# Attention on one core: other first loads, one last store, blank matmuls over a longer stretch, and a replanned order of work

## The chip, the cores and the metric

The kernel runs on one core of one Trainium2 chip. The metric is the device time of one execution in microseconds (us), as the median of several runs. A profile of one execution stands beside it; its times are counted from the start of its span, which is a little shorter than the device time. The engines are named as the profile names them: PE is TensorE's matmul, PEld its weight load, ACT is ScalarE, DVE is VectorE, POOL is GpSimd and SP is SyncE, which here only issues transfers (DMAs).

## The reference

Grouped-query attention over 8 batches, 8 query heads, 2 key/value heads, 1024 positions and a head dimension of 64, in float32:

```python
scores = scale * np.matmul(q_group, k_group.transpose(0, 1, 3, 2))
scores_max = np.max(scores, axis=-1, keepdims=True)
attn = np.exp(scores - scores_max)
attn = attn / (np.sum(attn, axis=-1, keepdims=True) + 1e-08)
output[:, q_start:q_end, :, :] = np.matmul(attn, v_group)
```

There are 64 (batch, query head) jobs. Each has a 1024 x 1024 score matrix, its exponential, a sum over each row, and a product with v. The inputs are small (0.1 times a normal draw), so the kernel leaves out the maximum.

## The kernel before, in words

A job's scores are made transposed, keys on the partitions. One score pair is two matmuls (line 754) of 128 keys against 512 queries each, for the two halves of the queries, and fills one of three slots in PSUM (the tiles sp0 to sp2, 128 x 1024 float32). A job has 8 such pairs, so there are 512 in all. Each pair's exponential is made by one of two engines:

- ScalarE makes it with one ACTIVATE of 128 x 1024 (line 767), which writes the bfloat16 tile pt.
- VectorE makes it in integer steps: a scale and offset to a 16-bit pattern (line 778, "yt"), and then for two pairs together a mask for the mantissa (line 785, "zt"), a mask for the exponent (line 792, "et") and a product (line 801). GpSimd makes the last 256 columns of some of the products (line 728). For all but the last two jobs, et and zt both go into the product with v, so a pair made this way costs TensorE two value matmuls where ScalarE's costs one.

The value product (line 819) has the exponential as weights and v, with a column of ones that gives the row sums, as the moving side (65 columns). Eight pieces of 128 queries make a job. Seven pieces at a time collect in one of two PSUM banks (ops0, ops1), and VectorE divides them by the sums (lines 875 and 884) into the ring tile ost, from which SP stores whole jobs (line 888). The last job collects in a score slot (line 840), and its store is cut in two halves, on SP's and on ScalarE's queue (line 852).

Queries and keys reach their transposed layout by DMA: GpSimd's queue casts them to bfloat16 in DRAM (lines 529 and 537), and SP's queue issues transposing loads (lines 562 and 572). The first job takes a faster path. Its q and k are loaded directly by four DMAs (line 594: k block 0 and then the upper half of q on ScalarE's queue, the lower half of q and then k blocks 1 to 3 on SP's), cast (line 615), transposed by matmuls against an identity (line 627) and copied out of PSUM (lines 636 to 638). After the first score pair, `rest_k0` transposes k blocks 1 to 3 and copies them with one VectorE instruction (line 643), and `swap_k0` makes the swapped-halves copy of k (line 653). Before the first real matmul, TensorE runs six blank matmuls of 512 columns and three of 128 on a zero tile (line 604).

The order of all of it is written out before the kernel is built, by a planner (the class Plan). It keeps a clock for each engine, made of constants for the durations (M_...), and at each step chooses for TensorE between a score for ScalarE ("A"), a score for VectorE ("D"), a piece of the value product ("V", up to GRAIN matmuls at once), a piece of the last job ("L"), a wait ("W") and a blank matmul of 128 columns ("F"). Where there is a choice it plays the alternatives forward over HORIZON and weighs ScalarE's and VectorE's idle time, TensorE's waste and its progress by W_A, W_D, W_P and W_LAG. MXD limits how many pairs of a job go to VectorE (two); every MORE-th job may have one more. M_START is the time at which the planner takes the first score to be possible. Blank matmuls within the plan are allowed until M_FILL and only before the first value matmul:

```python
elif t < M_FILL and s.pc == 0 and s.done == 0:
    kind = "F"
```

The planned events are then emitted in order of time, each engine having its own instruction stream and semaphores between them; transfers are emitted at set leads before the planned time of their use.

Of the kernel before, what the change touches and what calls it, by code (L numbers as in the profile page):

```python
# [8 lines left out]


M_START = 5400
M_SWAP = 1500
M_Q1 = 3400
M_QSTEP = 2700
M_WARM = 6400
M_FILL = 12000
M_DUMMY = 110
M_SEE = 51
M_PAIR = 226
# [15 lines left out]

M_GAP = 120
M_RUNWAY = 1800
M_BACK = 3000
M_WAIT = 150
M_TOL = 300  # L40

HORIZON = 9000
W_A = 1.0
W_D = .28
W_P = .3
W_LAG = 20
INF = float("inf")
PB = 7
NPIECE = 8
GRAIN = 3  # L50
MXD = 2
MORE = 12
TAIL = 2
# [59 lines left out]
class Plan:  # L113
# [5 lines left out]
    def __init__(self, nj, npt, nct, nyt):  # L119
        self.nj, self.npt, self.nct, self.nyt = nj, npt, nct, nyt  # L120

        self.last = (nj - 1) * NPIECE
        self.groups = [(i, min(i + PB, self.last)) for i in range(0, self.last, PB)]
        self.groups += [(self.last, self.last + NPIECE)]
        self.group_of = [g for g, (lo, hi) in enumerate(self.groups) for _ in range(lo, hi)]
        self.qready = [M_START] + [M_START + M_Q1 + M_QSTEP * j for j in range(nj - 1)]
        s = State()
        s.nxt = [0] * nj
        s.dcount = [0] * nj
        s.pcnt = [0] * nj  # L130
        s.pmax = [0] * nj
        s.a_of = [0] * nj
        s.mms = [8] * nj
        s.slot = [M_START, M_START, M_START + M_SWAP - 600]
        s.aq, s.dq = [], []
        s.out = [M_START, M_START]
        s.norms, s.gq = [], []
        s.tP = s.tA = M_START
        s.tD = M_START + M_SWAP
        s.tG = M_START + 9000  # L140
        s.endA, s.endD = s.tA, s.tD
        s.idleA = s.idleD = s.waste = 0
        s.mode = s.open = s.dlast = None
        s.dend = 0
        s.chains, s.heads, s.nch = [], {}, 0
        s.pc = s.done = s.a = s.used_p = s.used_c = 0
        s.lastp, s.left, s.spare = [INF] * 8, 8, None
        s.placed = 0
        s.end = False
        s.ev = []  # L150
        self.run(s)
# [118 lines left out]

    def pick_d(self, s):
        for j in range(s.a, min(self.nj, s.a + 3)):
            if s.nxt[j] < 8 and s.dcount[j] < MXD + (j % MORE == 1) and self.qready[j] <= s.tP:
                return j
        return None

    def choices(self, s):

        t, nj = s.tP, self.nj
        while s.a < nj and s.nxt[s.a] == 8:
            s.a += 1
        a = s.a
        cold = 2 if t < M_WARM else 1
        free = [x for x in (0, 1, 2) if s.slot[x] <= t]
        runway = s.tA - t + M_ACT * len(s.aq)
        slack = runway - cold * M_PAIR - M_PTAIL - (M_SWITCH if s.mode != "s" else 0)
        can_a = a < nj and len(s.aq) < 2 and self.qready[a] <= t and s.used_p < self.npt  # L290
        dj = None
        held = len({ch.id for ch in s.chains} | {x[1].id for x in s.gq})
        if not s.dq and held < self.nyt and (s.open or s.used_c < self.nct):
            if max(s.tD - t, 0) + sum(ch.left() for ch in s.chains) < M_BACK:
                dj = self.pick_d(s)
        s.free, s.dj = free, dj
        can = []
        kind = None
        if free:
            can += ["A"] * can_a + ["D"] * (dj is not None)  # L300
            if dj is not None:
                if not can_a:
                    kind = "D"
                elif len(free) > 1 or slack <= M_GAP or s.mode == "s":
                    other = min(s.slot[x] for x in (0, 1, 2) if x != free[0])
                    late = not s.aq and other > s.tA - M_PAIR - M_PTAIL + M_TOL
                    kind = "A" if late or slack <= M_PAIR else "D"
            elif can_a:
                full = len(free) > 1 or s.mode == "s"
                if slack <= M_GAP or (full and runway < M_RUNWAY):  # L310
                    kind = "A"
        pv = s.pc < self.last and (
            s.done > 0
            or (
                s.pcnt[s.pc // NPIECE] == 8
                and s.pmax[s.pc // NPIECE] <= t
                and s.out[self.group_of[s.pc] % 2] <= t
            )
        )
        wait = s.mode == "s" and any(t < x <= t + M_WAIT for x in s.slot)  # L320
        can += ["V"] * pv + ["W"] * (wait and (can_a or dj is not None))
        if kind is None:
            if wait and (dj is not None or (can_a and runway < M_RUNWAY + M_WAIT)):
                kind = "W"
            elif pv:
                kind = "V"
            elif s.left and a == nj and (free or s.spare is not None) and min(s.lastp) <= t:
                kind = "L"
            elif t < M_FILL and s.pc == 0 and s.done == 0:
                kind = "F"  # L330
            else:
                kind = "W"
        return kind, [x for x in can if x != kind]

    def turn(self, s, mode):
        if s.mode != mode:
# [4 lines left out]
    def pe(self, s, kind):  # L341
        t, nj = s.tP, self.nj
        if kind in "AD":
            self.turn(s, "s")
            sl = s.free[0]
            j = s.a if kind == "A" else s.dj
# [38 lines left out]
        elif kind == "L":  # L385

            if s.spare is None:
                s.spare = s.free[0]
                s.slot[s.spare] = INF
            self.turn(s, "v")  # L390
            c = min(range(8), key=lambda c: s.lastp[c])
            s.lastp[c] = INF
            s.left -= 1
            s.note(s.tP, "pvl", c, s.left, None)
            s.tP += NPIECE * M_MM
            if not s.left:
                s.norms.append((s.tP + M_PVTAIL, "rec", self.last, self.last + NPIECE))
        elif kind == "F":
            s.note(s.tP, "dummy", None, None, None)
            s.tP += M_DUMMY  # L400
            s.mode = "v"
        else:
            x = min([x for x in s.slot if x > t] + [max(s.tA, t) + 1, max(s.tD, t) + 1, t + 60])
            s.tP = max(x, t + 5)
            s.waste += s.tP - t
# [44 lines left out]
def kernel(  # L450
# [64 lines left out]
    warm = kvp.tile([128, HS], BF16, name="warm")  # L515
    ident = kvp.tile([128, 128], BF16, name="ident")
    nc.vector.memset(warm, 0.0)  # L517
    nc.vector.memset(va[:, :, :, :, D : D + 1], 1.0)
    kt, qt, qd, kd, vs = {}, {}, {}, {}, {}

    def cast_q(j):
# [65 lines left out]
    kt[(0, 0)] = ktp.tile([128, 2, HS], BF16, name="kt")  # L587
    qt[0] = qp.tile([128, 1, HS], BF16, name="qt")
    k0, q0 = kt[(0, 0)], qt[0]
    for e, x, lo, hi in (  # L590
        (nc.scalar, "k", 0, 1), (nc.sync, "q", 0, 2), (nc.scalar, "q", 2, NH), (nc.sync, "k", 1, NH)
    ):
        src = {"q": q, "k": k}[x][0, 0]
        e.dma_start(out=f32[x][:, lo:hi], in_=rows(src, True)[:, lo:hi])  # L594
    cast_q(1)
    make_identity(nc, ident)
    cast_q(2)
# [1 line left out]
    new_bank(0)  # L599
    new_bank(1)  # L600

    def dummy(n, cols):
        for _ in range(n):
            nc.tensor.matmul(  # L604
                ops[1][:, 0:cols], lhsT=warm[:, 0:128], rhs=warm[:, 0:cols], start=True, stop=True
            )

    dummy(6, HS)
    dummy(3, 128)

    def place(e, x, lo, hi):
        to, src = b16[x][:, lo:hi], f32[x][:, lo:hi]
# [27 lines left out]

    def rest_k0():
        turn("k", 1, NH, s2[:, 0])
        nc.vector.tensor_copy(out=k0[:, 0, 128:HS], in_=s2[:, 0, 128:HS])  # L643

    def swap_k0():
        for c in range(NH):
# [26 lines left out]
    for x in [e for e in plan.ev if e[1] == "norm"]:  # L673
        lo, hi = x[2]
        for j in range(NJ - 1):
            if lo < (j + 1) * NPIECE <= hi:
                ev.append((x[0] + 700, "store", None, j, None))
        if lo >= plan.last:
            ev.append((x[0] + 1, "half", 0, None, None))
            ev.append((x[0] + 2, "half", 1, None, None))  # L680
    order = {id(e): i for i, e in enumerate(ev)}
    ev.sort(key=lambda e: (e[0], order[id(e)]))

# [29 lines left out]
    for when, kind, x, j, c, *cols in ev:  # L713
# [110 lines left out]
                    stop=(i == len(every) - 1),  # L824
                )
        elif kind == "dummy":
            dummy(1, 128)
        elif kind == "pvl":
            b, h = divmod(NJ - 1, H)
            first = j == NC - 1  # L830
# [2 lines left out]
            for i in range(NPIECE):  # L833
# [5 lines left out]
                for n, (ci, p) in enumerate(every):  # L839
# [5 lines left out]
                        stop=(j == 0 and n == len(every) - 1),  # L845
                        skip_group_check=True,
                    )
        elif kind == "half":
            b, h = divmod(NJ - 1, H)
            r = plan.last % RING  # L850
            lo = x * 64
            (nc.scalar if x else nc.sync).dma_start(
                out=rows(out[b, h], True)[lo : lo + 64],
                in_=ost[lo : lo + 64, r : r + NPIECE, :].rearrange(
                    "p (s two) d -> p s (two d)", two=2
                ),
            )
        elif kind in ("rec", "norm"):
            lo, hi = x
            n = hi - lo  # L860
# [24 lines left out]
        elif kind == "store":  # L885
            b, h = divmod(j, H)
            r = j * NPIECE % RING
            ins = nc.sync.dma_start(
                out=rows(out[b, h], j == 0),
                in_=ost[:, r : r + NPIECE, :].rearrange("p (s two) d -> p s (two d)", two=2),  # L890
            )
            stores.append((when, ins))
# [30 lines left out]
```

The softmax here doesn't subtract the row's maximum and nothing guards it: scores larger than these inputs give would overflow.

## Time and profile before

| What | Value |
|---|---|
| Median of three runs | 365.02 us |
| Runs | 363.99, 365.12, 365.02 us |
| Profiled execution, device time | 363.19 us |
| Its span | 361.4 us |
| Its mean granted TensorE clock | 0.992 |
| PE, DVE, ACT busy | 97% each |
| POOL busy | 33% |
| ACTIVATE for the exponential | 378, mean 1057 ns each |
| VectorE's first step (yt) | 134, mean 1212 ns each |
| Value matmuls | 2976 from pt, 1056 from zt, 1040 from et |
| Score matmuls | 1024 |

Consecutive ACTIVATEs overlap in the record, so the mean duration of one is more than its share of the engine's busy time (348.6 us for 378). In a row of groups, the numbers after the bar are the busy time and the mean duration, and after the second bar the idle time just before these instructions with what ended it. In the chain of work that ended last and in the timeline, a row has its start, its length and what it is. In a table of stages, each row has the stretch and its length, then for PE, PEld, DVE, ACT and POOL the busy time and the number of instructions, then the granted TensorE clock as a share of full speed, the share of DMA time and the GB/s moved.

### The profile page before, as it was taken

Reading aid. Unit: us, or ns where it says so; the run is one execution under the profiler, and the core shown is the slowest. Engines: PE = TensorE matmul, PEld = TensorE weight load, DVE = VectorE, ACT = ScalarE, POOL = GpSimd, SP = SyncE. Lnnn points to the kernel's source line nnn. Section 1 sums busy time; section 2 is a strip of 40 time slices with the busy share of each in tenths; the row PEclk is TensorE's granted clock in tenths of the full one; section 3 lists DMA queues with packets and bytes.
Section 4 is the critical chain, followed back from the end, with each engine's and each line's share of the span. In section 5 each row is a group of like instructions: output and inputs, shape, how many; then the busy total and the mean of one; then the engine's idle time right before and its main releaser. Section 6 shows DMA issues by size and latency. Waiting matters only on the chain.

```text
span 361.4 us, 14113 instructions
## 1 busy us (share of the span) xinstructions
PE 349.0 (97%) x6213; PEld 222.2 (61%) x6213; DVE 349.4 (97%) x491; ACT 351.1 (97%) x382; POOL 120.8 (33%) x202
## 2 busy tenths in 40 slices
PE   7799999999999999999999999999999999999994
PEld 3256666566666666666665666666666666666664
DVE  4999999999999999999999999999999999999993
ACT  5999999999999999999999999999999999999994
POOL 4224443333334233343422333343324424432000
PEclk9989999999999999999999999999999999999998
DMA  6724767376696857469565676969468555853323
GB/s 160 134 41 77 188 108 147 84 139 143 110 161 115 166 103 162 99 123 172 125 143 108 124 137 111 171 119 150 107 129 149 122 118 122 175 132 48 88 61 89
DMA packets 89565, 44.82 MB, mean 124 GB/s; under 512 B 46032, under 2 KB 87888, under 8 KB 88272
## 3 DMA queue, kind: packets, MB, share of 16 engines
q1 hardware_dynamic: 86144, 33.37, 40.7%
q0 software_dynamic: 2992, 10.23, 21.1%
q8 instruction: 48, 0.79, 0.9%
q10 hardware_dynamic: 368, 0.33, 0.3%
q14 instruction: 13, 0.11, 0.1%
HBM read 25.17 MB, written 27.00 MB: 144 GB/s over the span
## 4 chain that ended last, share of the span: by engine, by line
PE 43%; DVE 35%; ACT 18%; issue 1%; DMA 1%; ACTq 0%; DVEq 0%
PE ops L819 24%; PE sp L754 18%; ACT pt L767 18%; DVE yt L778 16%; DVE zt L801 6%; DVE et L792 4%; DVE ost L884 4%; DVE zt L785 4%; DVE rec L875 1%; DMA q<-in_q_dram 1%; PE sp L840 1%; PE sp L627 0%; DVE kt L643 0%; DVE qt L637 0%; ACTq L594 0%
## 5 line engine op out<-in xcount | busy, mean ns | idle before, releaser
L767 ACT ACTIVATE pt<-sp 128x1024 bf16<-128x1024 f32 x378 | 348.6, 1057 | 2.2 <-PE sp L754 2.1
L819 PE MATMUL ops<-va,pt 128*128 128x65 bf16 x2976 | 186.2, 194 | 0.0
L754 PE MATMUL sp<-qt,kt 64*128 64x512 bf16 x1024 | 173.7, 384 | 6.3 <-ACT pt L767 3.4
L778 DVE TENSOR_SCALAR yt<-sp 128x1024 uint16<-128x1024 f32 x134 | 162.5, 1212 | 0.9 <-PE sp L754 0.9
L819 PEld LDWEIGHTS <-pt 128*128 128x128 bf16 x2976 | 136.3, 98 | 41.1 <-issue 41.1
L819 PE MATMUL ops<-va,zt 128*128 128x65 bf16 x1056 | 134.4, 195 | 0.0
L819 PE MATMUL ops<-va,et 128*128 128x65 bf16 x1040 | 128.5, 195 | 0.0
L728 POOL TENSOR_TENSOR zt<-yt,zt 128x256 bf16<-128x256 bf16 x102 | 68.2, 668 | 139.2 <-DVE zt L801 50.5
L819 PEld LDWEIGHTS <-et 128*128 128x128 bf16 x1040 | 84.8, 98 | 30.8 <-issue 30.8
L819 PEld LDWEIGHTS <-zt 128*128 128x128 bf16 x1056 | 88.2, 98 | 12.1 <-issue 12.1
L754 PEld LDWEIGHTS <-kt 64*128 64x128 bf16 x1024 | 45.5, 93 | 44.7 <-issue 22.1
L801 DVE TENSOR_TENSOR zt<-yt,zt 128x1536 bf16<-128x1536 bf16 (+1 forms) x67 | 67.8, 1012 | 0.0
L529 POOL DMA_DIRECT2D qd<-in_q_dram x62 | 35.5, 573 | 40.4 <-PE sp L754 38.0
L785 DVE TENSOR_SCALAR zt<-yt 128x2048 uint16<-128x2048 uint16 x67 | 45.2, 675 | 0.4
L792 DVE TENSOR_SCALAR et<-yt 128x2048 uint16<-128x2048 uint16 x67 | 45.2, 674 | 0.0
L884 DVE TENSOR_TENSOR ost<-ops,rec 128x448 f32<-128x448 f32 x72 | 44.1, 613 | 0.2
L554 POOL CAST va<-vs 128x512 bf16<-128x512 f32 x16 | 9.8, 612 | 23.6 <-DVE et L792 5.9
L875 DVE RECIPROCAL rec<-ops 128x7 f32<-128x7 f32 x72 | 13.9, 193 | 0.6 <-PE ops L819 0.5
L537 POOL DMA_DIRECT2D kd<-in_k_dram x15 | 8.2, 544 | 5.2 <-PE sp L754 3.6
L604 PE MATMUL ops<-warm 128*128 128x128 bf16 (+1 forms) x37 | 5.7, 295 | 1.2 <-DVE warm L517 1.2
L604 PEld LDWEIGHTS <-warm 128*128 128x128 bf16 x37 | 2.7, 108 | 4.8 <-issue 3.6
L615 ACT ACT_TABLE_LOAD x1 | 1.3, 1283 | 1.7 <-PEq L907 1.7
(31 smaller groups left out, 16.5 us busy)
## 6 DMA issues: line engine op xcount, KB each, us to landing
out_dram<-ost SPq DMA_DIRECT2D x63, 256.0 KB, 3.4
qd<-in_q_dram POOLq DMA_DIRECT2D x63, 128.0 KB, 3.5
vs<-in_v_dram SPq DMA_DIRECT2D x16, 256.0 KB, 4.5
kd<-in_k_dram POOLq DMA_DIRECT2D x15, 128.0 KB, 3.2
kt<-kt SPq DMA_DIRECT2D x30, 64.0 KB, 2.9
qt<-qd SPq DMA_TRANSPOSE x63, 3.7
kt<-kd SPq DMA_TRANSPOSE x15, 4.7
k<-in_k_dram SPq DMA_DIRECT2D x1, 192.0 KB, 3.4
```

The source lines that it names most:

```text
L529: return nc.gpsimd.dma_start(out=t.rearrange("(a x) d -> a (x d)", x=4), in_=q[b, h].rearrange("(a x) d -> a (x d)", x=8),)
L554: return nc.gpsimd.tensor_copy(out=va[:, b * G + g, :, :, 0:D], in_=vs.pop((b, g)).rearrange("p c (two d) -> p c two d", two=2),)
L728: gps = nc.gpsimd.tensor_tensor(out=z, in0=flat(yt[j])[:, c, 1024 - GC :], in1=z, op=ALU.mult)
L754: now = nc.tensor.matmul(sps[x][:, half, :], lhsT=t[lo : lo + D, c // NH, ci % NH * 128 : (ci % NH + 1) * 128], rhs=qt[j][lo : lo + D, 0, ...
L767: exps.append(nc.scalar.activation(out=p, in_=where_s[(j, c)], func=AF.Exp, scale=scale))
L778: vec = nc.vector.tensor_scalar(out=yt[ch][:, i, :, :], in0=where_s[c], scalar1=EXP_A, scalar2=EXP_B, op0=ALU.mult, op1=ALU.add,)
L785: vec = nc.vector.tensor_scalar(out=zt[j][:, 0:c], in0=yt[j][:, 0:c], scalar1=0x7F, scalar2=0x3F00, op0=ALU.bitwise_and, op1=ALU.bitwise_or,)
L792: vec = ins = nc.vector.tensor_scalar(out=et[j][:, 0:c], in0=yt[j][:, 0:c], scalar1=0x7F80, scalar2=None, op0=ALU.bitwise_and,)
L801: vec = nc.vector.tensor_tensor(out=z, in0=flat(yt[j])[:, 0:c, 0 : cols[0]], in1=z, op=ALU.mult)
L819: nc.tensor.matmul(ops[plan.group_of[x] % 2][:, lo : lo + D + 1], lhsT=p[:, qs * 128 : (qs + 1) * 128], rhs=va[:, b * G + h // HPG, ci % N ...
L875: vec = nc.vector.reciprocal(out=to, in_=sums)
L884: vec = nc.vector.tensor_tensor(out=to, in0=o, in1=by, op=ALU.mult)
```

## The change

- First loads: k block 0 and, behind it, k blocks 1 to 3 on SP's queue, the latter held until VectorE's second memset is done; the whole of q in one load on ScalarE's queue.
- Three blank matmuls of 128 columns before the first transposes become one. The blank helper can write either bank.
- `rest_k0` copies k block 1 by itself, then blocks 2 and 3.
- Blank matmuls within the plan: wherever TensorE would wait in the first 40 us (planner's time) and no slot comes free within M_IDLE, and no longer only before the first value matmul. They write the bank that isn't collecting.
- The third VectorE pair of every twelfth job begins with the seventh job instead of the second.
- The last job's store is one DMA on SP's queue.
- Other constants of the planner: start times, HORIZON, the weights, GRAIN, M_BACK, M_TOL. The whole order of work is planned anew.

In the order that results, ScalarE has 379 exponentials (before: 378), VectorE 133 first steps (134), GpSimd 98 products (102); there are 41 blank matmuls after the first score (28), and 5064 value matmuls in pieces from the collecting banks (5072).

```diff
-M_START = 5400
-M_SWAP = 1500
+M_START = 5250
+M_KREST = 650
+M_SWAP = 1600
-M_FILL = 12000
+M_FILL = 40000
+M_IDLE = 350
-M_BACK = 3000
+M_BACK = 2500
-M_TOL = 300
-HORIZON = 9000
-W_A = 1.0
+M_TOL = 100
+HORIZON = 5500
+W_A = .72
-W_LAG = 20
+W_LAG = 0
-GRAIN = 3
+GRAIN = 2
...
-        s.slot = [M_START, M_START, M_START + M_SWAP - 600]
+        s.slot = [M_START, M_START + M_KREST, M_START + M_SWAP - 600]
...
-            if s.nxt[j] < 8 and s.dcount[j] < MXD + (j % MORE == 1) and self.qready[j] <= s.tP:
+            if s.nxt[j] < 8 and s.dcount[j] < MXD + (j % MORE == MORE // 2) and self.qready[j] <= s.tP:
...
-            elif t < M_FILL and s.pc == 0 and s.done == 0:
+            elif t < M_FILL and all(x <= t or x > t + M_IDLE for x in s.slot + [self.other(s, t)]):
                 kind = "F"
...
+    def other(self, s, t):
+        return 0 if s.out[1 - self.group_of[s.pc] % 2] <= t else t + 1
...
-    for e, x, lo, hi in (
-        (nc.scalar, "k", 0, 1), (nc.sync, "q", 0, 2), (nc.scalar, "q", 2, NH), (nc.sync, "k", 1, NH)
-    ):
+    def load(e, x, lo, hi):
         src = {"q": q, "k": k}[x][0, 0]
-        e.dma_start(out=f32[x][:, lo:hi], in_=rows(src, True)[:, lo:hi])
+        return e.dma_start(out=f32[x][:, lo:hi], in_=rows(src, True)[:, lo:hi])
+    load(nc.sync, "k", 0, 1)
+    load(nc.scalar, "q", 0, NH)
+    rest = load(nc.sync, "k", 1, NH)
+    tc.add_manual_dep(rest.ins, ones.ins.name, Sync, reason="loads in time, not sooner")
...
     dummy(6, HS)
-    dummy(3, 128)
+    dummy(1, 128)
...
-        nc.vector.tensor_copy(out=k0[:, 0, 128:HS], in_=s2[:, 0, 128:HS])
+        for lo, hi in ((128, 256), (256, HS)):
+            nc.vector.tensor_copy(out=k0[:, 0, lo:hi], in_=s2[:, 0, lo:hi])
...
-            ev.append((x[0] + 1, "half", 0, None, None))
-            ev.append((x[0] + 2, "half", 1, None, None))
+            ev.append((x[0] + 1, "store", None, NJ - 1, None))
```

More of the change, by code (lines that the diff above doesn't have):

```diff
@@ L398, in pe @@
         elif kind == "F":
-            s.note(s.tP, "dummy", None, None, None)
+            s.note(s.tP, "dummy", 1 - self.group_of[s.pc] % 2, None, None)
             s.tP += M_DUMMY
@@ L517 @@
     nc.vector.memset(warm, 0.0)
-    nc.vector.memset(va[:, :, :, :, D : D + 1], 1.0)
+    ones = nc.vector.memset(va[:, :, :, :, D : D + 1], 1.0)
     kt, qt, qd, kd, vs = {}, {}, {}, {}, {}
@@ L600, with dummy @@
     new_bank(1)
-    def dummy(n, cols):
+    def dummy(n, cols, bank=1):
         for _ in range(n):
             nc.tensor.matmul(
-                ops[1][:, 0:cols], lhsT=warm[:, 0:128], rhs=warm[:, 0:cols], start=True, stop=True
+                ops[bank][:, 0:cols], lhsT=warm[:, 0:128], rhs=warm[:, 0:cols],
+                start=True, stop=True,
             )
     dummy(6, HS)
-    dummy(3, 128)
+    dummy(1, 128)
     def place(e, x, lo, hi):
@@ L826 @@
         elif kind == "dummy":
-            dummy(1, 128)
+            dummy(1, 128, x)
         elif kind == "pvl":
@@ L847 @@
                     )
[L848 to L857, printed above, removed]
         elif kind in ("rec", "norm"):
@@ L888 @@
             ins = nc.sync.dma_start(
-                out=rows(out[b, h], j == 0),
+                out=rows(out[b, h], j in (0, NJ - 1)),
                 in_=ost[:, r : r + NPIECE, :].rearrange("p (s two) d -> p s (two d)", two=2),
```

## The prediction

> **What bounds the kernel now.** I read the page's engine shares, then its rows, the chain that ended last, and the timeline of the two ends.
>
> ```profile
> PE 349.0 (97%) x6213; PEld 222.2 (61%) x6213; DVE 349.4 (97%) x491; ACT 351.1 (97%) x382; POOL 120.8 (33%) x202
> L767 ACT ACTIVATE pt<-sp 128x1024 bf16<-128x1024 f32 x378 | 348.6, 1057 | 2.2 <-PE sp L754 2.1
> L778 DVE TENSOR_SCALAR yt<-sp 128x1024 uint16<-128x1024 f32 x134 | 162.5, 1212 | 0.9 <-PE sp L754 0.9
> ```
>
> Three engines are full. ScalarE (ACT) is first among them: its 378 exponentials make 348.6 us of 361.4, so one costs 348.6/378 = 0.922, and they wait 2.2 in all. That wait and the two ends are nearly all that is not exponential. The chain and the timeline say where they lie (start, length, what).
>
> ```profile
> 1.18 3.08 DMA q<-in_q_dram
> 4.29 0.30 DVE q L614
> 5.70 0.39 PE sp L754 x2
> 6.40 0.57 DVE kt L643
> 7.01 0.62 PE sp L754 x4
> ...
> 6.13 1.02 ACT L767 ACTIVATE pt<-sp 128x1024 bf16<-128x1024 f32 x1 [0.84 <-PE sp L754]
> 7.66 1.94 ACT L767 ACTIVATE pt<-sp 128x1024 bf16<-128x1024 f32 x2 [0.51 <-PE sp L754]
> ...
> 21.99 1.97 ACT L767 ACTIVATE pt<-sp 128x1024 bf16<-128x1024 f32 x2 [0.47 <-PE sp L754]
> ```
>
> The first exponential waits for the second half of q; the second starts 7.66 - 6.13 = 1.53 after it, 0.61 more than its price, because the scores stand behind one 0.57 us copy of three key blocks. The one at 21.99 waits again. The stages around it, with TensorE's granted clock as the column after the five engines:
>
> ```profile
> 13.00:15.00 2.00, 1.18 (x8) 0.29 (x7) 1.97 (x3) 2.00 (x4) 0.00 (x0) 1.00 0.82 96
> 15.00:17.00 2.00, 1.17 (x10) 0.30 (x9) 2.00 (x3) 2.00 (x4) 0.67 (x1) 1.00 0.72 183
> 17.00:19.00 2.00, 1.48 (x10) 0.46 (x8) 2.00 (x3) 2.00 (x3) 0.67 (x1) 0.74 0.58 124
> 19.00:21.00 2.00, 1.80 (x20) 0.85 (x17) 2.00 (x4) 2.00 (x3) 0.14 (x1) 0.50 0.03 4
> 21.00:23.00 2.00, 2.00 (x37) 1.28 (x34) 1.78 (x2) 1.53 (x3) 1.23 (x3) 0.91 0.00 0
> ```
>
> TensorE (PE) works 1.2 of each 2 us from 13 to 17; the clock then falls to half, and the first value matmuls run on it. Time at half clock: 2 x (0.26 + 0.50 + 0.09)/0.5 = 3.4 us. The end:
>
> ```profile
> 354.03 2.08 ACT L767 ACTIVATE pt<-sp 128x1024 bf16<-128x1024 f32 x2
> 356.71 0.21 DVE L875 RECIPROCAL rec<-sp 128x8 f32<-128x8 f32 x1 [1.13 <-PE sp L840]
> 357.67 0.52 SPq L852 DMA_DIRECT2D out_dram<-ost  x1
> 357.67 0.56 ACTq L852 DMA_DIRECT2D out_dram<-ost  x1
> ```
>
> **What the Trainium skill says.** "TensorE: Matmul & The Clock Gate", Part 1, has the clock halve after a window of about 3.4 us with too little matmul work, and return after a busy one, the windows running free of the kernel. The trace agrees in length (3.4 us) and shows that 1.2 of 2 us is too little, while 1.75 to 1.91 of 2 (7 to 13 us, where blank matmuls run) kept full clock. "DMA: Bandwidth & Descriptors", Issuing engines are not separate DMA queues: loads issued from several engines share the same 16 DMA engines, and only issue time is saved. Here a second issue on a queue costs 0.43 to 0.45 us. Its Anatomy of one DMA prices a transfer at 2.0 us plus bytes over 436 GB/s: an estimate of 2.6 for 256 KB and 2.3 for 128 KB. The trace is slower, 2.4 to 3.1 for 128 KB and 3.4 for the stores of 256 KB, and decides.
>
> **The change part by part.** Counts are from the changed instruction order, durations from the rows above, all against the 361.4 us span; that execution took 363.19, so 1.8 lie outside, and the three runs were 363.99 to 365.12. I apply the difference to their median, 365.02.
>
> First loads. q comes as one 256 KB load, first on ACT's queue at 0.74, instead of two whose second was issued at 1.18 and landed at 4.26. The rest of k now waits for a DVE memset (over at 1.72), so it doesn't compete with q; what it delays on SP's queue, the v load, waited until 3.93 anyway. Saved: 0.44 of issue, and competition. Added: the pace of 256 KB, 128/436 = 0.3, and both casts wait for the whole. I take landing at 3.6 to 3.9. From there ScalarE's cast 0.42, matmuls on q 0.4, DVE's copies 0.42 and 0.21, score and eviction as before (6.13 - 5.70): first exponential near 5.85. Gain 0.3, between 0.5 gained and 0.2 lost (landing as late as now, with the longer cast in the path). The two fewer blank matmuls of 0.11 before the first transposes make room for this. The late k rest lands near 1.75 + 3.4 = 5.15; its cast (0.51) ends at 5.7, and TensorE reaches its transposes only after the first score, so it costs nothing. POOL's order keeps its first three casts of q.
>
> The copy of k is split: the score for ScalarE's second exponential now needs one block, at the 0.28 of the row for such a copy instead of 0.57, and this score is the second in the order, no longer the third (0.22). The extra instruction's fixed cost lies beside the first exponential. With that one starting earlier, 0.05 of the 0.61 may stay: gain 0.55 (0.25 to 0.61).
>
> Blank matmuls: 41 instead of 28, now up to the first value matmul, in gaps where all three score slots are busy. At 0.05 us each they fill idle time; a score that becomes free waits for at most one or two. They lift 13 to 17 us from 1.2 of 2 towards 1.5 or more. If the clock holds, the 0.47 wait goes, with the extra step of 0.2 before it (from 20.36, as 15 exponentials began at 7.66, to 21.99 is 1.63 against 0.92): gain 0.7. If not, nothing (0 to 0.9).
>
> New plan (all planner constants, and the head with a third VectorE pair is every twelfth from the seventh, not from the second): 379 exponentials on ScalarE for 378, 133 pairs on VectorE for 134: a loss of 0.92. VectorE loses one 1.21 us pass and half of a pair of 0.67 us passes, 1.2 + 0.7 = 1.9, and keeps the multiplies (4 fewer go to POOL, which waits 139 us and doesn't bind): say 1.7. TensorE has 8 fewer value matmuls (0.03 each), but turns between scores and value matmuls 622 times for 612, at 0.32 for one pair against 0.54 for two, thus 0.10 a turn: +0.75 net. The chain gives DVE 35% and PE 43% of the span: -1.7 x 0.35 + 0.75 x 0.43 = -0.3. Other waits that a new order makes can't be read from before; I bound this term at 1.5 gained and 1.0 lost.
>
> Last store: one of 256 KB on SP for two of 128 KB. The ACT queue's took 2.7, SP's 2.4; one stream adds 0.3 to SP's and drops the later queue: 0 to 0.3 gained, 0.3 lost at worst. I take 0.1 gained.
>
> Sum: -0.3 - 0.55 - 0.7 + 0.92 - 0.3 - 0.1 = -1.0. The clock windows run free, so other executions may hold more of the half clock than the profiled one, the lower of those shown; for that I take 0.2 more: -1.2, so 363.8 us.
>
> **Rivals.**
> The gains cancel: the clock still drops, since the window that matters may hold the gaps the blanks don't reach, and q lands no earlier. Then -0.55 + 0.92 - 0.3 - 0.1 = 0.0, and the rest of the blanks' promise 0.2: 364.8. For it: after 20 us ScalarE's chain ends at 68, then PE and DVE own it, so early gains could be eaten by slack. Against: an exponential lost at the start is never made up, with ScalarE at 97%.
>
> More than the sum: the order also removes waits hidden in the exponentials. Their durations run from 1017 to 1177 ns around one price of 0.922; 3 ns less of each gives 379 x 0.003 = 1.1. With the other parts: -2.1, 362.9.
>
> Slower: value matmuls taken two at a time, more turns, make scores late for ScalarE all along. The chain's last 30 us are PE alone, score and value matmuls alternating without a gap. It decides against the kernel from 1.2 + 1.1 = 2.3 us of late scores, 6 ns for each of 379 exponentials; at 7 ns, 2.7 - 1.2 = +1.5: 366.5. Against: ScalarE's recorded wait from 22 to 345 us is 0.9 in all.
>
> **How the numbers follow.** About 0.3%, 1.1 us, is what a measurement of this kernel can tell from no change: faster is below 363.9, slower above 366.1. The worked sum 0.50, its own range 362.9 to 364.7, of which 0.36 below 363.9; cancelled 0.20; more 0.18; slower 0.12. Faster 0.54, same 0.34, slower 0.12. The range 362.4 to 365.7 leaves out most of the slower case and the ends.
>
> **What would show it.** First exponential near 5.85 and the second 0.92 to 0.97 later; clock 1.00 from 13 to 23 us and no ScalarE wait at 20 to 22; 379 exponentials at 0.922 or less; one last store that lands 2.4 to 2.8 after its issue. Wrong if the mean exponential is above 0.925, if q lands after 4.2, or if the clock dips later.

## The result, and the profile after

The kernel after takes 361.91 us in the median of six executions (361.48 to 363.69), the kernel before 364.91 on the same chip (363.86 to 365.12). The ratio is 0.9933, with a 95% interval of 0.9908 to 0.9958, so the change makes it faster by 0.67%, some 2.4 us. The two medians lie 3.0 us apart; the ratio agrees with the means of the same executions, 362.2 and 364.6, and sizes below follow the ratios. A later comparison (a_same, nine executions of the kernel after: 362.67 us) gave 0.9936 [0.9913, 0.9958].

The two profiled spans differ by much less, 361.37 and 360.84 us. The experiments explain why. From the page of after, the lines that answer those shown of before:

```profile
PE 350.8 (97%) x6216; PEld 224.0 (62%) x6216; DVE 347.2 (96%) x491; ACT 351.7 (97%) x383; POOL 116.1 (32%) x198
L777 ACT ACTIVATE pt<-sp 128x1024 bf16<-128x1024 f32 x379 | 349.1, 1064 | 1.7 <-PE sp L764 1.5
L788 DVE TENSOR_SCALAR yt<-sp 128x1024 uint16<-128x1024 f32 x133 | 161.7, 1216 | 1.2 <-PE sp L764 1.2
```

There is one exponential more, at 349.1/379 = 0.921 us, and ScalarE waits 0.5 less. Its start, from the timeline of ScalarE:

```profile
5.08 0.52 ACT L625 ACTIVATE k<-k 128x384 bf16<-128x384 f32 x1
6.29 1.02 ACT L777 ACTIVATE pt<-sp 128x1024 bf16<-128x1024 f32 x1 [0.68 <-PE sp L764]
7.83 20.50 ACT L777 ACTIVATE pt<-sp 128x1024 bf16<-128x1024 f32 x22 [0.52 <-PE sp L764]
```

The wait at 21.99 us has gone: 22 exponentials follow one another from 7.83, and the timeline shows no wait among them. But the first is not earlier than before (6.29 for 6.13), and the second still follows it by 1.54. The stages where the clock fell before:

```profile
13.00:15.00 2.00, 1.61 (x15) 0.76 (x13) 2.00 (x4) 2.00 (x3) 0.06 (x1) 1.00 0.91 136
15.00:17.00 2.00, 1.56 (x15) 0.71 (x14) 1.97 (x3) 2.00 (x3) 0.11 (x1) 1.00 0.32 64
17.00:19.00 2.00, 1.70 (x17) 0.78 (x14) 2.00 (x3) 2.00 (x4) 0.94 (x2) 1.00 0.46 107
19.00:21.00 2.00, 1.73 (x22) 0.93 (x20) 2.00 (x3) 2.00 (x4) 0.29 (x1) 1.00 0.14 32
21.00:23.00 2.00, 2.00 (x48) 1.44 (x44) 2.00 (x3) 2.00 (x3) 1.18 (x2) 1.00 0.00 0
```

From 13 to 19 us TensorE is busy for 1.6 to 1.7 of each 2 us where it was 1.2 to 1.5, and the clock stays at 1.00. The end:

```profile
357.13 0.69 DVE L884 TENSOR_TENSOR ost<-sp,rec 128x512 f32<-128x512 f32 x1
357.86 0.34 SPq L888 DMA_DIRECT2D out_dram<-ost  x1
```

The last division ends 0.18 us later than before (357.82 for 357.64), and yet the span is 0.5 shorter: from the issue of the last store to the end it is 360.84 - 357.86 = 2.98, against 361.37 - 357.67 = 3.70.

One caution for reading. The clock column shows 1.00 from the start, because the trace's clock record begins with the clock's first rise, at 4.3 us in the profile of before and at 9.6 in that of after. The matmuls show it (PE's timeline after):

```profile
5.63 0.61 PE L764 MATMUL sp<-qt,kt 64*128 64x512 bf16 x2 [0.72 <-ACT k L625]
6.17 0.50 PE L637 MATMUL sp<-ident,k 128*128 128x128 bf16 x3
8.57 0.82 PE L613 MATMUL ops<-warm 128*128 128x128 bf16 x6
10.50 0.45 PE L613 MATMUL ops<-warm 128*128 128x128 bf16 x5
10.96 0.39 PE L764 MATMUL sp<-qt,kt 64*128 64x512 bf16 x2
```

A score pair takes 0.61 us at 5.63 and 0.39 at 10.96; before's first pair, at 5.70, took 0.39. So the profiled execution of before had the better start of the two. Below, a late rise is a first rise of the clock at 8.9 us or later. All profiles here have one except those of before (4.3) and a_best (6.7).

### The profile page after: what moved, and what is told of

Its sections match the earlier page's. It is cut to its first block, busy times and chain, and to the rows that moved or that the text cites. A ratio compares the mean times of both kernels' runs of the same rounds, so it can differ in the third digit from the quotient of the medians.

```text
span 360.8 us, 14112 instructions
## 1 busy us (share of the span) xinstructions
PE 350.8 (97%) x6216; PEld 224.0 (62%) x6216; DVE 347.2 (96%) x491; ACT 351.7 (97%) x383; POOL 116.1 (32%) x198
## 4 chain that ended last, share of the span: by engine, by line
ACT 73%; PE 23%; DMA 1%; DVE 1%; issue 1%
ACT pt L777 73%; PE ops L829 12%; PE sp L764 10%; DMA k<-in_k_dram 1%; PE sp L850 1%; DVE yt L788 0%; PE ops L613 0%; DVE ost L884 0%; DVE et L802 0%; PE ops L660 0%; ACT k L625 0%; PE sp L637 0%; DVE warm L523 0%; DVE rec L875 0%; DVE va L524 0%
## 5 line engine op out<-in xcount | busy, mean ns | idle before, releaser
L777 ACT ACTIVATE pt<-sp 128x1024 bf16<-128x1024 f32 x379 | 349.1, 1064 | 1.7 <-PE sp L764 1.5
L829 PE MATMUL ops<-va,pt 128*128 128x65 bf16 x2984 | 183.2, 194 | 0.0
L829 PEld LDWEIGHTS <-pt 128*128 128x128 bf16 x2984 | 134.4, 97 | 45.1 <-issue 45.1
L829 PE MATMUL ops<-va,zt 128*128 128x65 bf16 x1048 | 128.8, 194 | 0.0
L738 POOL TENSOR_TENSOR zt<-yt,zt 128x256 bf16<-128x256 bf16 x98 | 65.5, 668 | 144.2 <-DVE et L802 47.4
L829 PEld LDWEIGHTS <-zt 128*128 128x128 bf16 x1048 | 86.4, 97 | 2.4 <-issue 2.4
L764 PEld LDWEIGHTS <-kt 64*128 64x128 bf16 x1024 | 46.9, 93 | 42.9 <-issue 19.6
L811 DVE TENSOR_TENSOR zt<-yt,zt 128x1536 bf16<-128x1536 bf16 (+2 forms) x67 | 67.1, 1002 | 0.0
L795 DVE TENSOR_SCALAR zt<-yt 128x2048 uint16<-128x2048 uint16 (+1 forms) x67 | 45.8, 684 | 0.5
L535 POOL DMA_DIRECT2D qd<-in_q_dram x62 | 33.6, 543 | 35.3 <-PE sp L764 30.9
L802 DVE TENSOR_SCALAR et<-yt 128x2048 uint16<-128x2048 uint16 (+1 forms) x67 | 44.9, 670 | 0.0
```

What stands on the lines that cost most here:

```text
L535: return nc.gpsimd.dma_start(out=t.rearrange("(a x) d -> a (x d)", x=4), in_=q[b, h].rearrange("(a x) d -> a (x d)", x=8),)
L738: gps = nc.gpsimd.tensor_tensor(out=z, in0=flat(yt[j])[:, c, 1024 - GC :], in1=z, op=ALU.mult)
L764: now = nc.tensor.matmul(sps[x][:, half, :], lhsT=t[lo : lo + D, c // NH, ci % NH * 128 : (ci % NH + 1) * 128], rhs=qt[j][lo : lo + D, 0, ...
L777: exps.append(nc.scalar.activation(out=p, in_=where_s[(j, c)], func=AF.Exp, scale=scale))
L795: vec = nc.vector.tensor_scalar(out=zt[j][:, 0:c], in0=yt[j][:, 0:c], scalar1=0x7F, scalar2=0x3F00, op0=ALU.bitwise_and, op1=ALU.bitwise_or,)
L802: vec = ins = nc.vector.tensor_scalar(out=et[j][:, 0:c], in0=yt[j][:, 0:c], scalar1=0x7F80, scalar2=None, op0=ALU.bitwise_and,)
```

## The experiments

The theories, as the expectations name them. **C**, clock: what the gain has beyond the worked sum lies in windows of half clock early on, which most executions of before have more of than the profiled one. **P**, plan: the new order of work is better all along. **S**, store: the one last store gives most. Each ratio is to the kernel before, on the same chip, with its 95% interval. The kernels ran in three groups on three chips, so kernels of different groups are compared by these ratios: after stands at 0.9933 and 0.9936 (a_same). Each interval reaches 0.002 to 0.003 to either side, so the times alone tell none of the variants of after clearly from after; the sizes rest on the traces as well, and each trace is one execution.

**a_same: after once more**, as the measure for a_oldloads, b_fill and a_bridge.

> The kernel after once more, as the measure for the others of this group. Theory C: its executions lie in two or three clusters about 1 us apart, by the time at which TensorE's clock first rises (4.3 us in the profile of before, 9.6 in that of after, 12.7 in the repeat of before), and none has half clock between 13 and 22 us; ratio 0.993.

No execution had a mean clock under 0.999. Two clusters show, 361.8 and 362.3 to 362.8 us; the first rise in its profile is at 9.3 us.

**b_same: before once more.** No edit.

> The kernel before once more, for the spans and mean clocks of several executions. Theory C (clock: the part of the gain beyond the worked sum lies in windows of half clock in the first 25 us, of which the profiled execution of before had one, and others have more): spans of 361 to 364 us with mean clocks from 0.992 down to 0.985, the longer ones at the lower clocks. Theory P (plan: the new order is better by over 2 us all along): the clock is about 0.992 in all and the time doesn't follow it.

364.81 us; its profiled execution took 366.72. ScalarE's timeline in that profile:

```profile
6.74 1.02 ACT L767 ACTIVATE pt<-sp 128x1024 bf16<-128x1024 f32 x1 [1.44 <-PE sp L754]
8.87 1.02 ACT L767 ACTIVATE pt<-sp 128x1024 bf16<-128x1024 f32 x1 [1.10 <-PE sp L754]
10.05 1.02 ACT L767 ACTIVATE pt<-sp 128x1024 bf16<-128x1024 f32 x1 [0.16 <-PE sp L754]
11.56 1.02 ACT L767 ACTIVATE pt<-sp 128x1024 bf16<-128x1024 f32 x1 [0.48 <-PE sp L754]
24.64 1.02 ACT L767 ACTIVATE pt<-sp 128x1024 bf16<-128x1024 f32 x1 [0.79 <-PE sp L754]
26.23 2.10 ACT L767 ACTIVATE pt<-sp 128x1024 bf16<-128x1024 f32 x2 [0.57 <-PE sp L754]
```

The stages of the same profile (columns as before, the clock after the five engines):

```profile
16.00:20.00 4.00, 2.38 (x14) 0.58 (x12) 3.97 (x5) 4.00 (x6) 1.29 (x2) 0.94 0.26 47
20.00:24.00 4.00, 3.46 (x33) 1.85 (x32) 4.00 (x6) 3.85 (x5) 0.72 (x2) 0.50 0.14 33
24.00:28.00 4.00, 4.00 (x55) 2.33 (x55) 2.20 (x3) 2.74 (x3) 1.17 (x2) 0.71 0.23 33
```

Here the clock first rises at 12.7 us, and is half again for 6.8 us from 19.5. ScalarE waits for scores seven times by 28 us (the row left out, at 12.74, has another 0.16), and its thirty-first exponential starts at 38.27 instead of 34.85. That is the same program, 3.4 us apart. Of the 75 executions of before that stand beside this group, 28 have a mean clock of 0.991 or less and take 364.6 to 366.9 us; the 0.992 of the profile goes with 363.0 to 363.5. That supports one half of theory C: the profile from which I predicted was among the better starts, and 66 of the 75 took longer than its 363.19. The other half, that most executions have more half clock than it, isn't shown: 28 of 75 isn't most, and the mean clock is a rough guide. It leaves out the half clock before the first rise and takes in half clock at the very end, when TensorE has finished; the longest executions have 0.990 or 0.991, and those at 0.984 and 0.985 take 365.1 to 365.8.

**b_fill: before with 26 more blanks**, at the planned gaps after score pairs; the other instructions keep their order.

```diff
+    busy = [e for e in plan.ev if e[1] in ("score", "dummy", "pv")]
+    blanks, first = {}, next(e[0] for e in busy if e[1] == "pv")
+    for e, f in zip(busy, busy[1:]):
+        if e[1] == "score" and f[1] == "score" and 12000 < e[0] < first:
+            blanks[e[3], e[4]] = max(0, int((f[0] - e[0] - 226 - 100) / 110))
...
+            dummy(blanks.get((j, c), 0), 128)
```

> The kernel before with 26 more blank matmuls after score pairs before the first value matmul; its order of work is otherwise unchanged. Theory C: no half clock between 13 and 27 us, 0.7 to 1.5 us faster than before (ratio 0.996 to 0.998). Theory P: at most 0.3 faster.

363.96 us, ratio 0.9979 [0.9960, 0.9998]: 0.8 us faster. Its profiled execution has its first rise at 12.6 us, like that of b_same, which makes the two a matched pair:

```profile
16.00:20.00 4.00, 3.67 (x33) 1.85 (x31) 3.93 (x5) 4.00 (x5) 1.13 (x2) 1.00 0.37 63
20.00:24.00 4.00, 3.67 (x57) 2.27 (x56) 4.00 (x5) 4.00 (x6) 0.95 (x3) 1.00 0.14 33
24.00:28.00 4.00, 3.96 (x63) 2.31 (x59) 3.97 (x6) 4.00 (x5) 1.74 (x3) 1.00 0.23 33
```

And ScalarE's timeline of b_fill, its last row before 28 us:

```profile
12.78 15.69 ACT L774 ACTIVATE pt<-sp 128x1024 bf16<-128x1024 f32 x17 [0.16 <-PE sp L760]
```

The clock stays up and ScalarE runs on from 12.78. The fifth exponential starts at 12.78 (b_same 12.74) and the thirty-first at 36.57 (38.27): the half clock costs 1.7 us where it lasts 6.8 us, and blanks alone take it away. In the mean they are worth less, since not every execution of before is like b_same; two of b_fill's 22 executions still have a mean clock of 0.991 and 0.992.

**a_nofill: after without its 41 planned blanks.**

```diff
         elif kind == "dummy":
-            dummy(1, 128, x)
+            pass
```

> The kernel after without the 41 blank matmuls inside the plan; all else is in the same order. Theory C: 1.5 to 2.5 us slower than after (363.4 to 364.4), mean clock below 0.995, half clock in the profile between 10 and 22 us. Theory P and theory S (the last store gives most): within 0.5 us of after, 361.9.

362.97 us, ratio 0.9954 [0.9935, 0.9972], about 0.7 us slower than after: less than C expected, more than P and S. In its profile the clock first rises at 19.4 us, and yet the thirty-first exponential starts at 35.36, only 0.67 later than in after. The 0.7 is not clear of noise (the intervals overlap). Of the 15 executions with a mean clock of 0.976 to 0.990, 11 take 362.0 to 362.7, about as long as after; the seven at 0.999 or 1.000, the profiled one among them, take 363.3 to 365.1. Before at 0.985 takes 365.1 to 365.4. So, as far as mean clocks tell it, after without blanks bears half clock behind the first rise better than before does; b_newplan, below, shows that the order alone doesn't.

**a_halves: after with two half stores; b_onestore: before with one store.** One undoes what the other does alone (b_onestore's single store keeps the row layout that the halves had). The edit of a_halves, without the lines that issue a half:

```diff
-            ev.append((x[0] + 1, "store", None, NJ - 1, None))
+            ev.append((x[0] + 1, "half", 0, None, None))
+            ev.append((x[0] + 2, "half", 1, None, None))
...
```

> The kernel after with the last store cut in two halves on two queues again. Theory S (the one store ends 0.8 us sooner, as the two profiles say from the issue to the end): 362.6 to 362.8, and 3.7 us from issue to the end of the span. Theories C and P, with my predicted 0.1: 361.9 to 362.1.

> The kernel before with the last job's store as one DMA on SP's queue; nothing else. Theory S (0.67 us from the issue of the store to the end, as the kernel after with two halves showed): 0.7 us faster than before, ratio 0.998, and 3.0 us from issue to the end of the span instead of 3.7. My predicted 0.1 us: the same as before, 3.6 us.

a_halves: 363.36 us, 0.9961 [0.9941, 0.9981], about 0.9 us slower than after. b_onestore: 364.29 us, 0.9985 [0.9967, 1.0003], 0.5 us faster than before, not clear of no change. The intervals don't settle the size, the traces do: from the issue to the end of the span 361.62 - 357.97 = 3.65 in a_halves and 2.98 in after (360.84 - 357.86), 3.70 in before and 2.93 in b_onestore. SP's own waits at the end (total, times, longest), of a_halves:

```profile
SPq L929 <- DMA out_dram<-ost: 1.7, 1, 1.7
```

and of after:

```profile
SPq L918 <- DMA out_dram<-ost: 1.2, 1, 1.2
```

Half a microsecond is that wait. The issue is the rest: two halves take 0.54 and 0.57 us to issue, the single store 0.34. The records of the transfers show why the wait is longer. In before, SP's half moves its data from 358.85 to 359.67 and ScalarE's, issued at the same time, only from 359.46 to 360.00; they land 2.4 and 2.7 us after the issue. The single store of after begins 0.9 us after its issue and lands 2.0 after it. The store is worth 0.7 us in before as in after. That is what theory S expected of the store itself, but not most of the 2.4.

**a_oldplan and b_newplan: the order of work by itself.** a_oldplan is after with the order of before and the blanks of b_fill; b_newplan is before with the new constants and nothing else (its rule for blanks is the old one, so its order is near to that of after, not the same). From the edit of b_newplan:

```diff
-M_START = 5400
-M_SWAP = 1500
+M_START = 5250
+M_KREST = 650
+M_SWAP = 1600
...
-HORIZON = 9000
-W_A = 1.0
+HORIZON = 5500
+W_A = .72
...
-W_LAG = 20
+W_LAG = 0
...
-GRAIN = 3
+GRAIN = 2
...
```

> The kernel after with the order of work of before (its constants, its rule for blanks), plus 26 blank matmuls after score pairs before the first value matmul. It has 378 exponentials. Theory P: over 2 us slower than after, 363.9 to 364.9. Theory C: the plan is worth nearly nothing, 361.3 to 362.3.

> The kernel before with the constants of the new plan only (start times, weights, horizon, pieces of two, the head with a third VectorE pair); old loads, old copy, old rule for blanks, two half stores. It has 379 exponentials, and its order is close to that of after, not the same. Theory P2 (the new order begins with ScalarE's second exponential sooner and runs the rest at 0.921 us per exponential instead of 0.923): 0.5 to 0.9 us faster than before, ratio 0.9975 to 0.9985. My sum for this term, with the extra exponential: 0.6 us slower.

a_oldplan: 363.26 us, 0.9959 [0.9938, 0.9979], about 0.9 slower than after. b_newplan: 365.34 us, 1.0025 [1.0003, 1.0047], 0.9 slower than before. Theory P fails: the order is not worth 2 us. Taking it out (a_oldplan) cost less than P and more than C expected; put in alone (b_newplan), it loses, as my sum for it said (0.6). What the traces say in parts:

- The first exponentials. In executions with a late first rise, the second follows the first by 2.12 us with the old order and the old copy (b_same, b_fill and b_onestore alike), by 1.69 in b_newplan, by 1.97 in a_oldplan, and by 1.54 in after.
- The rate. From the thirty-first to the last start it is 0.9211 us per exponential in after, a_halves, a_nofill and a_same, and 0.9224 to 0.9228 in before, b_same and a_oldplan. Over 348 that is 0.45 to 0.6 us, so of the extra exponential's 0.92 the order gives half back. In b_newplan it is 0.9202, and nearly all comes back.
- The end. In a_oldplan the last store takes 3.42 from issue to end, instead of 2.98: an earlier store, issued at 356.25, is still under way beside it and lands only at 360.15. That is 0.4 of the 0.9.

In profiles with the same course of the clock (first rise at 12.4 and 12.7, half clock for 6.8 us from 19.2 and 19.5), b_newplan's span is 364.8 and b_same's 364.9, and its thirty-first exponential starts at 38.05, hardly sooner than b_same's 38.27. So the order alone doesn't bear the half clock better. Why its median is 0.9 us worse is open: 13 of its 14 executions have a mean clock of 0.993 or less, but so have 42 of the 52 of before beside it, and how often each order meets a bad start wasn't separated from the order itself.

**a_oldloads: after with the first loads of before**, and its three blanks ahead of the transposes.

```diff
...
-    load(nc.sync, "k", 0, 1)
-    load(nc.scalar, "q", 0, NH)
-    rest = load(nc.sync, "k", 1, NH)
-    tc.add_manual_dep(rest.ins, ones.ins.name, Sync, reason="loads in time, not sooner")
+    for e, x, lo, hi in (
+        (nc.scalar, "k", 0, 1), (nc.sync, "q", 0, 2), (nc.scalar, "q", 2, NH), (nc.sync, "k", 1, NH)
+    ):
...
-    dummy(1, 128)
+    dummy(3, 128)
```

> The kernel after with the four first loads of before and three blank matmuls ahead of the first transposes; all else as after. My step on the loads: 0.3 us slower than after. The rival (q as one load lands no sooner, and k block 0 lands 0.6 later, 3.9 instead of 3.3): the same as after or 0.2 faster.

362.43 us, 0.9945 [0.9923, 0.9967]: by times not told apart from after. ScalarE's timeline has the first exponential at 6.74:

```profile
6.74 1.02 ACT L774 ACTIVATE pt<-sp 128x1024 bf16<-128x1024 f32 x1 [1.44 <-PE sp L761]
```

In after it is 6.29 and in a_same 6.44; all three have a late rise. The other late-rise profiles agree: with the old loads 6.67 to 7.26 (b_newplan, b_same, b_fill, b_onestore), with the new ones 6.31 to 6.42 (a_oldplan, a_nosplit, a_halves, a_nofill), and 6.69 in a_bridge, for a reason given there. I put the loads, with the two blanks, at 0.3 to 0.45 us.

**a_nosplit and a_best: what the second exponential waits for.** a_nosplit copies k blocks 1 to 3 at once. a_best moves the eight matmuls of the swapped k behind the second score pair, and has the blanks of a_bridge, below.

```diff
-        for lo, hi in ((128, 256), (256, HS)):
-            nc.vector.tensor_copy(out=k0[:, 0, lo:hi], in_=s2[:, 0, lo:hi])
+        nc.vector.tensor_copy(out=k0[:, 0, 128:HS], in_=s2[:, 0, 128:HS])
```

```diff
                 rest_k0()
+            if len(where_s) == 2:
                 swap_k0()
```

> The kernel after with k blocks 1 to 3 copied by one VectorE instruction again. My step (the score for the second exponential waits for 0.28 us of copy instead of 0.57): 0.3 us slower than after, the second exponential 1.8 us after the first. The rival (the eight matmuls of the swapped k stand ahead of that score on TensorE, and end no sooner than either copy): the same as after, 1.54 us.

> The kernel after with the blanks of the bridge (one more before the first transposes, six before the first score), and with the eight matmuls of the swapped k moved behind the second score pair. The rival of my copy step: the second exponential follows the first by 1.0 to 1.3 us instead of 1.54, and the time is 0.3 to 0.5 us under after. If the copy alone set it: 1.54 and the same as after.

a_nosplit: 363.00 us, 0.9942 [0.9924, 0.9960], by times as after; a_best: 362.23 us (361.98 to 362.40), 0.9939 [0.9916, 0.9962]. ScalarE's timeline of a_nosplit:

```profile
6.33 1.02 ACT L776 ACTIVATE pt<-sp 128x1024 bf16<-128x1024 f32 x1 [0.86 <-PE sp L763]
8.03 1.94 ACT L776 ACTIVATE pt<-sp 128x1024 bf16<-128x1024 f32 x2 [0.67 <-PE sp L763]
```

and of a_best:

```profile
6.29 1.02 ACT L779 ACTIVATE pt<-sp 128x1024 bf16<-128x1024 f32 x1 [0.82 <-PE sp L765]
7.50 1.94 ACT L779 ACTIVATE pt<-sp 128x1024 bf16<-128x1024 f32 x2 [0.18 <-PE sp L765]
```

The steps are 1.70, 1.54 (after) and 1.20. The split copy is worth 0.16 us, not the 0.28 of its shorter piece; the swapped-k matmuls were the next thing in the way, worth up to 0.34 (a_best's clock also rose earlier, at 6.7 us, so part of this may be the clock's). The gain in time that I expected of a_best, 0.3 to 0.5 us, isn't seen.

**a_bridge: after with blanks over TensorE's early idle time.**

```diff
-    dummy(1, 128)
+    dummy(2, 128)
...
     turn("k", 0, 1, s0[:, 0])
+    dummy(6, 128)
```

> The kernel after with one more blank matmul before the first transposes, and six between the transpose of k block 0 and the first score, where TensorE stood idle from 4.92 to 5.63 us. Theory C: TensorE is now busy enough for its clock to rise at the end of the first window whatever the phase, at the latest at about 7.7 us, and the slow cluster of executions goes: 0.4 to 1.0 us faster than after in the median. The rival (the phase decides alone, or the blanks stand before the first score): the same, or 0.3 slower.

361.77 us (six executions, one at 363.25), 0.9925 [0.9896, 0.9955]. Its profiled execution still has the first rise at 9.9 us, so the blanks do not bring it about whenever the windows fall (my expectation was 7.7 at the latest). ScalarE's timeline shows another thing: the rest of k landed 1.2 us later than in after, and its cast, which stands ahead of the first exponential on ScalarE, held that back to 6.69.

```profile
6.26 0.52 ACT L625 ACTIVATE k<-k 128x384 bf16<-128x384 f32 x1 [1.26 <-DMA k<-in_k_dram]
6.69 1.00 ACT L778 ACTIVATE pt<-sp 128x1024 bf16<-128x1024 f32 x1
```

Neither a_bridge nor a_best is shown to beat after: all three intervals overlap.

## Why the prediction was right, and where its size was off

The direction and the sign of every step held. The size didn't: the forecast was 1.2 us of gain, and the ratio says 2.4, with an interval of 1.5 to 3.4. The ratio on 365.02 gives 362.6. That is 0.2 inside the stated range but below the worked sum's own, 362.9 to 364.7, and the median of after itself, 361.91, lies 0.5 below the stated range. Step by step:

- **First loads, 0.3.** q was cast from 3.73, within the 3.6 to 3.9 I gave, and the rest of k from 5.08, against 5.15. The first exponential came at 6.29, not 5.85: the step took the score and the transposes at full clock, and after's profile had half clock until 9.6. Against before with a late rise the gain is there: 6.74 in b_same, 6.29 to 6.44 in after. That the late rest of k costs nothing held in after; in a_bridge it landed 1.2 us later and held the first exponential back. The price by bytes in Anatomy of one DMA is stated there for transfers through GpSimd, which these are not: q's 256 KB landed 3.0 us after its issue, where the price gives 2.6.
- **Second exponential, 0.55.** Between the two profiles nothing, between late-rise executions 2.12 - 1.54 = 0.58. That the size fits is partly luck: I worked it out at full clock, where no profile of after shows it, and its division was wrong. The new place of the score in the order gives 2.12 - 1.70 = 0.42 (I had 0.22), the copy 0.16 (I had 0.28). The matmuls of the swapped k, ahead of that score on TensorE, were not in the sum.
- **Blank matmuls, 0.7 for the one half-clock window, and 0.2 for executions with more of them.** The first is what the profile pair shows: the step of 1.63 us at 20.36 became 0.90. Together they are 0.9, and b_fill measured 0.8 (0.1 to 1.5) for blanks alone, so in the mean they were about right. Single executions differ far more: b_same and b_fill put two windows at 1.7 us together. I saw that the profiled execution was below all three timed runs and didn't ask how far below the ordinary one it lay: the mean of the 75 is 364.5, its own time 363.19.
- **New plan, 0.92 less 0.3.** In the traces of after 0.92 less 0.45 to 0.6 for the rate. After without blanks bears half clock better than before (a_nofill), though the order alone doesn't (b_newplan); which part does stays open.
- **Last store, 0.1.** It gave 0.7: this is the term most off. I took one stream for two of half the size as a matter of bytes, and put its landing at 2.4 to 2.8 us after the issue; it landed after 2.0, and the later half of before after 2.7. The Trainium skill's "DMA: Bandwidth & Descriptors", Issuing engines are not separate DMA queues, says a second queue saves issue time only; here not even that was saved, since each half took longer to issue than the whole.

Put together, the parts as measured are 0.3 to 0.45 for the loads, 0.58 for the second exponential, 0.8 for the blanks and 0.7 for the store, less 0.3 to 0.5 for the plan. That is 1.9 to 2.2, against the 2.4 of the times and the 1.2 forecast; the store alone is 0.6 us of the 1.2 that the forecast lacked. It is a rough sum, since most parts come from single late-rise executions.

The account of the profiles closes. From b_same to after: the start, up to the thirty-first exponential, gives 38.27 - 34.69 = 3.6. From there to the last exponential's start after needs 0.3 more (320.5 for 320.2, one exponential more). Its tail to the last division is 0.1 shorter and the store 0.7: 4.1 in sum, and 364.9 - 360.8 = 4.1. From the profiled before it is 0.2 gained at the start, 0.5 lost from there to the last exponential, and 0.8 gained in tail and store: 0.5, as 361.37 - 360.84.

The rival in which the gains cancel fell with the clock at 1.00; the one with waits hidden in the exponentials had the nearest number, 362.9, but its reason was only half true, 1.3 to 1.7 ns each instead of 3; the slower one did not come: the mean exponential fell from 0.922 to 0.921 with more turns and pieces of two. One of the chances was also too high: a worked sum centred on 363.8 has near half of its 0.50 below 363.9, not 0.36.

## What to carry to other kernels

Look at several executions before pricing a start: where TensorE works at part load early on, one profile can be better than the next of the same program (here by 3.4 us at the thirty-first exponential), and a change that removes the sensitivity can gain more than that profile shows. Blank matmuls in TensorE's gaps were cheap insurance here. Nothing hid the last store of this kernel, so its issue and its landing counted in full: try one store before two.

## What the runs showed of the hardware

- TensorE's first rise of clock came anywhere from 4.3 to 19.4 us in the profiles of these near-alike starts. "TensorE: Matmul & The Clock Gate", Part 1, of the Trainium skill says that the windows run free of the kernel; the half-clock stretches here, 3.4 and 6.8 us, are one and two of its 3.4 us windows. The trace starts its clock record only at the rise, so the early half clock has to be read from the matmuls (0.61 us a score pair for 0.39).
- The recorded changes of the clock lie on a grid of 3.41 us (in before 4.30, 17.95 and 21.37), and early in this kernel a change goes with how busy PE was in the grid window just ahead of it. The clock fell after windows with PE busy 1.77 (before), 1.99 (b_newplan), 2.02 (b_same) and 2.13 us (b_onestore). Near the same place after has 2.58 and 2.85 and b_fill 3.09, and it stayed up; the least that kept it in the first 60 us is 2.20 (before, 4.30 to 7.71). So the section's idle window need not be idle: these were more than half busy.
- At half clock, the clock rose after grid windows with PE busy 3.10 us or more and not after less (after, 2.80 to 6.22: 2.54). So where TensorE's early gaps fall on the grid moves the first rise. Neither boundary is a general rule: 3.15 did not raise it once (a_nofill, 5.77 to 9.18), and at the end 1.73 kept it (a_best, 354.87 to 358.29).
- A store of 128 partitions took 0.34 us to issue and landed 2.0 us after it (after, a_same, b_onestore). Of two 64-partition halves issued together on SP's and ScalarE's queues, each took 0.52 to 0.57 to issue, and they landed after 2.4 and 2.7, the second moving its data when the first had nearly done (before, b_same, a_halves).
